# RWKV heads in one layout of full tiles: the second head's operands in reversed order, both heads' systems on the diagonal of one tile

## The chip, the cores and the metric

One core of a Trainium2 chip runs the whole program; the metric is device time in microseconds of one execution. PE in the rows is TensorE's matrix products, PEld its weight loads, DVE is VectorE, ACT ScalarE, POOL GpSimd, SP the engine whose queue issues the DMAs.

## What is computed

One residual layer over 16 learned and 1024 given tokens of 1024 channels, in float32. A normalised input goes through one projection of 61 tiles of 128 channels; three groups of heads mix over time; their outputs go through one output projection, a norm and the residual. The group in question is RWKV-7, 8 heads of 64 channels:

```python
def rwkv7_recurrence(r, w, k, v, a, b):          # (B, T, H, 64), state S (B, H, 64, 64)
    def step(state, inp):
        r_t, w_t, k_t, v_t, a_t, b_t = inp
        sa = jnp.einsum("bhvk,bhk->bhv", state, a_t)
        state = (state * w_t[:, :, None, :] + sa[..., None] * b_t[:, :, None, :]
                 + v_t[..., None] * k_t[:, :, None, :])
        return state, jnp.einsum("bhvk,bhk->bhv", state, r_t)
    ...
# called with a = -kk, b = kk * a, kk = l2_normalize(k * k_k) of each head
```

The others are gated DeltaNet (6 heads of 128) and Mamba-2 (12 heads of 64).

## The kernel before

**Projections.** A tile of 128 output channels takes 3 pieces of tokens x 8 blocks of input channels x 3 float32r products (high x high, high x low, low x high), 72 products `pj`. Its weights come by two DMAs, ScalarE rounds them (L149) and POOL computes the rest (L150); the next tile's weights are fetched when a tile has begun. Six `unit_a` (DeltaNet heads), four `unit_b` (pairs of RWKV heads) and two `unit_c` (Mamba) each project their tiles and then work them off in a scan over chunks; `unit_o` is the output projection.

**Order.** `schedule` writes out the order of all instructions by hand-made rules. Units are generators that yield after each step of a scan. A clock in microseconds of TensorE decides: when the result that a unit's next step waits for should be there, that step is emitted, otherwise the next product of a projection. `Meter` adds up the charges: a float32 product of n columns max(n, weight columns)/600 us, a projection product n/2400; and for the way back to TensorE, VectorE 0.25 + n/960, ScalarE 0.3 + n/1200 and POOL 0.3 + n/500 for n elements a partition, plus 0.3 a step. Instructions called through `nc.` are not charged. The plan is `a0 b0 b1 b2 c0 b3 a1 a2 a3 c1 a4 a5`. At most two scans run beside each other, each in a lane with two PSUM banks (`self.ps`). TensorE, like the other engines, takes what it was given in order.

**unit_b.** Chunks of 64 tokens, 17 of them; two heads lie on the partitions, 64 channels each. Per chunk `ar` = (a | r) and `bk` = (b | k) hold, along 128 columns, the operands of the token after and the token before, with their decays (VectorE). For each head a gram `bgm` (128 rows b, k by 128 columns a, r) is formed by one product of 64 rows and masked with `maskb`: four chunks a bank, a step for each head, ten steps. Its upper left 64x64 is a triangular system, scaled by `ib` = 1/|kappa|^2. The diagonal blocks of 32 go to DRAM and back to be solved (`solve32`), then pairs are merged to 64 by products of 32x32 (`bm`, through `bdd`), eight steps for two heads. Values are transposed into rows 64 to 127 of `uv`.

The scan has three steps a chunk. First `bsi` (bank `pq`): the state times `ar`, a full 128x128 product, then two products of 64x64 add k by a times the values for each head; ScalarE copies the upper half to `b_x`. Second `bu` (bank `pu`): two 64x64 products with the solved systems; VectorE scales the result by `ib` into rows 0 to 63 of `uv`. Third `bd`: a full product for the new state, which VectorE adds with the decay `b_wc` to what ScalarE has scaled (L817); and two products of 128 rows with 64 weight columns for the output, from `bgm` and `uv` into the lower half of `pq`, which ScalarE copies to `by` (L828).

Every call through a charged engine shows as L96, the line of `Meter`; go by the tile names.

## Time and profile before

| | |
|---|---|
| runs before (3) | 1534.42 us median, 1522.98 to 1535.38 |
| span of the profiled execution | 1518.0 us, first to last instruction; its own time outside the span is not listed |
| TensorE busy | 1427.0 us, 94% |
| VectorE, ScalarE, POOL busy | 1014.6, 647.8, 239.2 us |

Busy time of TensorE is the union of its products, whose ends are modelled; products overlap in the pipeline, so what one costs is seen in the distance between starts. A float32 product shows as two records, a float32r one as one.

### The profile page before, as it was taken

Reading aid. Unit: us, or ns where it says so; the run is one execution under the profiler, and the core shown is the slowest. Engines: PE = TensorE matmul, PEld = TensorE weight load, DVE = VectorE, ACT = ScalarE, POOL = GpSimd, SP = SyncE. Lnnn points to the kernel's source line nnn. Section 1 sums busy time; section 2 is a strip of 40 time slices with the busy share of each in tenths; the row PEclk is TensorE's granted clock in tenths of the full one; section 3 lists DMA queues with packets and bytes.
Section 4 is the critical chain, followed back from the end, with each engine's and each line's share of the span. In section 5 each row is a group of like instructions: output and inputs, shape, how many; then the busy total and the mean of one; then the engine's idle time right before and its main releaser. Section 6 shows DMA issues by size and latency. Waiting matters only on the chain.

```text
span 1518.0 us, 25931 instructions
## 1 busy us (share of the span) xinstructions
PE 1427.0 (94%) x9657; PEld 1259.6 (83%) x9657; DVE 1014.6 (67%) x2688; ACT 647.8 (43%) x1814; POOL 239.2 (16%) x227
## 2 busy tenths in 40 slices
PE   4999999999999999997999999999999999889897
PEld 3988878887888888987888898899998988678686
DVE  7549695476659456869735699745489967542573
ACT  5354351334434352443635534433456154532530
POOL 2122011011101111223101221102232111200100
PEclk9999998899999999999989999989999999999999
DMA  5221211111011121211111111101322111552851
GB/s 187 58 85 43 70 33 39 29 41 64 29 30 47 49 74 43 86 31 53 46 43 50 43 46 53 36 29 57 97 59 61 43 36 44 169 159 89 250 193 56
DMA packets 102880, 104.28 MB, mean 69 GB/s; under 512 B 37915, under 2 KB 70427, under 8 KB 102755
## 3 DMA queue, kind: packets, MB, share of 16 engines
q1 hardware_dynamic: 102755, 102.64, 22.0%
q8 instruction: 76, 1.25, 0.3%
q14 instruction: 49, 0.40, 0.1%
HBM read 85.00 MB, written 17.60 MB: 68 GB/s over the span
## 4 chain that ended last, share of the span: by engine, by line
PE 30%; DVE 14%; issue 5%; ACT 4%; DMA 3%; POOL 0%; SPq 0%; DVEq 0%; ACTq 0%; POOLq 0%
PE pj L96 14%; PE po L96 5%; DVE s_tmp L96 3%; DVE alb L96 2%; PE am L96 2%; DMA or<-in_w_out_dram 2%; PE bsi L96 1%; DVE aq L181 1%; DMA omrw<-d_mix 1%; PE aops L96 1%; PE ads L96 1%; DVE av L181 1%; PE aks L96 1%; PE av L96 1%; ACT clt L904 1%
## 5 line engine op out<-in xcount | busy, mean ns | idle before, releaser
L96 PE MATMUL pj<-hh,w 128*128 128x350 f32 (+8 forms) x2928 | 773.9, 338 | 0.2 <-ACT hh L261 0.2
L96 PEld LDWEIGHTS pj<-hh,w 128*128 128x128 f32 x2928 | 516.7, 192 | 13.2 <-issue 2.1
L96 PE MATMUL pj<-hl,w 128*128 128x350 f32 (+8 forms) x1464 | 493.4, 337 | 0.0
L150 POOL TENSOR_TENSOR w<-wr,w 128x512 fp32r<-128x512 f32 x122 | 173.6, 1424 | 870.3 <-ACT w L149 631.7
L96 PEld LDWEIGHTS pj<-hl,w 128*128 128x128 f32 x1464 | 281.3, 192 | 6.6 <-issue 0.9
L149 ACT CAST w<-wr 128x512 fp32r<-128x512 f32 x122 | 74.9, 615 | 75.8 <-PE pj L96 64.4
L96 PE MATMUL po<-ow,omw 128*128 128x512 f32 x408 | 95.5, 395 | 6.2 <-ACT omw L1064 3.7
L96 PEld LDWEIGHTS po<-ow,omw 128*128 128x128 f32 x408 | 77.2, 190 | 24.6 <-ACT omw L1064 4.4
L96 PE MATMUL po<-ow,ome 128*128 128x512 f32 x360 | 90.6, 399 | 4.6 <-ACT ow L1046 1.8
L96 PEld LDWEIGHTS po<-ow,ome 128*128 128x128 f32 x360 | 66.6, 188 | 20.1 <-POOL ow L1047 2.5
L96 DVE TENSOR_TENSOR alb<-alb,s_tmp 33x30 f32<-33x30 f32 (+9 forms) x180 | 71.2, 395 | 1.0
L96 DVE TENSOR_TENSOR s_tmp<-alb 33x30 f32<-33x30 f32 (+9 forms) x180 | 67.4, 375 | 0.9
L96 DVE TENSOR_TENSOR buv<-bu,b_ib 64x128 f32<-64x128 f32 x68 | 19.1, 281 | 69.5 <-PE bu L96 69.3
L96 PE MATMUL bsi<-buv,bgm 64*64 64x64 f32 (+1 forms) x528 | 61.5, 238 | 0.0
L96 PEld LDWEIGHTS bsi<-buv,bgm 64*64 64x64 f32 (+1 forms) x528 | 42.1, 139 | 17.5 <-issue 2.2
L828 ACT COPY by<-bsi 64x128 f32<-64x128 f32 x64 | 16.7, 262 | 82.3 <-PE bsi L96 81.8
L181 DVE SCALAR_TENSOR_TENSOR cbc<-pj,pack,cbc 128x346 f32<-128x346 f32 (+4 forms) x72 | 40.5, 568 | 14.3 <-ACT cbc L178 13.5
L96 DVE SCALAR_TENSOR_TENSOR b_s<-bd,b_wc,b_s 64x64 f32<-64x64 f32 x120 | 34.0, 283 | 23.2 <-PE bd L96 18.2
L96 DVE TENSOR_TENSOR blb<-blb,s_tmp 68x30 f32<-68x30 f32 (+14 forms) x120 | 46.5, 387 | 1.1
L96 PE MATMUL bgr<-bar,bbk 64*128 64x128 f32 x272 | 43.8, 328 | 2.6 <-DVE bbk L96 2.0
L1065 DVE TENSOR_TENSOR ome<-omre,ome 128x512 fp32r<-128x512 f32 (+2 forms) x40 | 22.4, 594 | 34.1 <-ACT ome L1064 34.0
L1047 POOL TENSOR_TENSOR ow<-or,ow 128x512 fp32r<-128x512 f32 x16 | 21.0, 1316 | 135.9 <-ACT ow L1046 135.9
(324 smaller groups left out, 2414.7 us busy)
## 6 DMA issues: line engine op xcount, KB each, us to landing
wr<-in_wt_dram SPq DMA_DIRECT2D x122, 256.0 KB, 2.6
or<-in_w_out_dram SPq DMA_DIRECT2D x32, 256.0 KB, 2.6
omrw<-d_mix SPq DMA_DIRECT2D x32, 256.0 KB, 4.7
clt<-d_cs SPq DMA_DIRECT2D x24, 256.0 KB, 4.5
omre<-d_mix SPq DMA_DIRECT2D x24, 256.0 KB, 4.2
btw<-d_tw SPq DMA_DIRECT2D x8, 544.0 KB
x<-in_x_dram SPq DMA_DIRECT2D x8, 512.0 KB, 7.0
oxr<-in_x_dram SPq DMA_DIRECT2D x8, 512.0 KB
```

Of the source, the lines that this page charges most:

```text
L96: return op(out, *args, **kw)
L149: nc.scalar.copy(w[:, 0], raw)
L150: nc.gpsimd.tensor_tensor(w[:, 1], raw, w[:, 0].bitcast(F32), SUB)
L181: nc.vector.scalar_tensor_tensor(acc[:, a + z: b], p[:, o + z - s: o + b - a - s], cw[:, 3 - s: 4 - s], acc[:, a + z: b], MUL, ADD)
L828: nc.scalar.copy(yt[hs[(c - 1) % 2], (c - 1) // 2, :], pq[64:128, 0:128])
L904: nc.scalar.activation(t[:, e, i], t[:, e, i], AF.Exp, bias=self.ncs[:, 1 + 4 * w + i, k + e: k + e + 1])
L1047: (nc.vector if k % 2 else nc.gpsimd).tensor_tensor(t[:, 1], raw, t[:, 0].bitcast(F32), SUB)
L1065: nc.vector.tensor_tensor(t[:, 1], raw, t[:, 0].bitcast(F32), SUB)
```

## The change

The first head of a pair keeps its order, the second has it reversed: `ar` is (a | r) on partitions 0 to 63 and (r | a) on 64 to 127, `bk` is (b | k) and (k | b). Gram products then are 64 rows by 64 weight columns by 128 columns, four a chunk instead of two, one for each quadrant of the array, into two banks: tile `bf` (program name `bgf`) holds what b meets, with both heads' systems on its diagonal; tile `be` (`bge`) what k meets. Each is masked with a mask of its own (`maskf`, `maske`, made once on POOL). Values stand off the diagonal of `uv`, which POOL clears first. A chunk's scan is five products of 128x128x128: `be` by `uv`, `ar` by the state, `bf` by `x`, `bt` by `uv`, and `bf` by the scaled `x` for the output. `x` is one of two cleared tiles `xb`; ScalarE writes its diagonal twice, first from `pq`, then scaled from `pu`, while VectorE writes the same solution to the diagonal of `uv`. Copies of diagonal parts are two instructions of 64x64 each. In the preparation the moves by halves are separate instructions, and r times its decay goes from VectorE to POOL. Merges take both heads in one step. Comments were removed throughout (not shown).

```diff
+masks = cp.tile([128, 2, 128], F32, tag="masks", name="masks")
+self.maskf, self.maske = masks[:, 0], masks[:, 1]
+lo, hi = slice(0, 64), slice(64, 128)
+for straight, turned, rows in ((self.maskf, self.maske, lo), (self.maske, self.maskf, hi)):
+    nc.gpsimd.tensor_copy(straight[rows], self.maskb[rows])
+    nc.gpsimd.tensor_copy(turned[rows, lo], self.maskb[rows, hi])
+    nc.gpsimd.tensor_copy(turned[rows, hi], self.maskb[rows, lo])
...
 ar, bk = ([self.one([128, 9 - i, 128], f"b{x}{p}_{i}") for i in range(2)] for x in ("ar", "bk"))
-ib = sm.tile([64, 17, 2], F32, tag="b_ib", name="b_ib")
+hs = (slice(0, 64), slice(64, 128))
+ib = sm.tile([128, 17], F32, tag="b_ib", name="b_ib")
 for i, (s, e) in enumerate(split):
     act.activation(bk[i][:, :, 0:64], k[:, s:e], AF.Square, scale=self.kk[:, p: p + 1])
 yield
 ps = self.ps(f"bn{p}")
 for c in range(17):
     pe.matmul(ps[0:64, 2 * c: 2 * c + 2], at_c(bk, c)[:, 0:64], self.blk[:, 0:65:64], start=True, stop=True)
-v.tensor_scalar(ib, ps[0:64, 0:34].rearrange("p (c h) -> p c h", h=2), EPS, None, ADD)
+for h in range(2):
+    v.tensor_scalar(ib[hs[h]], ps[0:64, h: 34: 2], EPS, None, ADD)
 v.reciprocal(ib, ib)
 for i, (s, e) in enumerate(split):
     kap, b_ = ar[i][:, :, 0:64], bk[i][:, :, 0:64]
     act.activation(kap, k[:, s:e], AF.Copy, scale=self.kk[:, p: p + 1])
     v.scalar_tensor_tensor(b_, at[:, s:e], 1.0, kap, ADD, MUL)
-    v.scalar_tensor_tensor(kap, kap, -1.0, e1[:, s:e, 0:64], MUL, MUL)
-    v.scalar_tensor_tensor(b_, b_, 0.5, cs[:, s:e, 1:], MUL, MUL)
+    for h in (1, 0):
+        v.scalar_tensor_tensor(ar[i][hs[h], :, hs[h]], kap[hs[h]], -1.0, e1[hs[h], s:e, 0:64], MUL, MUL)
+        v.scalar_tensor_tensor(bk[i][hs[h], :, hs[h]], b_[hs[h]], 0.5, cs[hs[h], s:e, 1:], MUL, MUL)
+        pool.tensor_tensor(ar[i][hs[h], :, hs[1 - h]], r[hs[h], s:e], e1[hs[h], s:e, 1:], MUL)
...
 for i, (s, e) in enumerate(split):
-    v.tensor_tensor(bk[i][:, :, 64:], k[:, s:e], cs[:, s:e, 1:], MUL)
-    v.tensor_tensor(ar[i][:, :, 64:], r[:, s:e], e1[:, s:e, 1:], MUL)
+    for h in range(2):
+        v.tensor_tensor(bk[i][hs[h], :, hs[1 - h]], k[hs[h], s:e], cs[hs[h], s:e, 1:], MUL)
 yield 11
 self.calm = False
-gms = [[self.one([128, 9 - i, 128], f"bgm{p}_{h}{i}") for i in range(2)] for h in range(2)]
-gm = lambda h, c: at_c(gms[h], c)
+bf, be = ([self.one([128, 9 - i, 128], f"b{x}{p}_{i}") for i in range(2)] for x in ("gf", "ge"))
 banks = ((1, 5), (5, 9), (9, 13), (13, 17), (0, 1))
-hs = (slice(0, 64), slice(64, 128))
 for s, e in banks:
-    for h in range(2):
-        ps = self.ps(f"bgr{p}_{h}{s}")
-        for c in range(s, e):
-            pe.matmul(ps[:, 128 * (c - s): 128 * (c - s) + 128], at_c(bk, c)[hs[h]], at_c(ar, c)[hs[h]], start=True, stop=True)
-        v.tensor_tensor(gms[h][s // 9][:, s % 9: s % 9 + e - s, :], ps[:, : 128 * (e - s)].rearrange("p (c t) -> p c t", c=e - s),
-                        bc(self.maskb, 1, e - s), MUL)
-        yield PIPE
+    pf, pg = self.ps(f"bgf{p}_{s}"), self.ps(f"bge{p}_{s}")
+    for c in range(s, e):
+        to = slice(128 * (c - s), 128 * (c - s) + 128)
+        for out, row, h in ((pf, 0, 0), (pf, 1, 1), (pg, 0, 1), (pg, 1, 0)):
+            pe.matmul(out[hs[row], to], at_c(bk, c)[hs[h], hs[row]], at_c(ar, c)[hs[h]], start=True, stop=True)
+    for out, ps, mask in ((bf, pf, self.maskf), (be, pg, self.maske)):
+        v.tensor_tensor(out[s // 9][:, s % 9: s % 9 + e - s, :], ps[:, : 128 * (e - s)].rearrange("p (c t) -> p c t", c=e - s),
+                        bc(mask, 1, e - s), MUL)
+    yield PIPE
 for h in range(2):
     for i, (s, e) in enumerate(split):
-        ab = gms[h][i][0:64, :, 0:64]
-        nc.vector.tensor_tensor(ab, ab, bc(ib[:, s:e, h], 2, 64), MUL)
+        ab = bf[i][hs[h], :, hs[h]]
+        nc.vector.tensor_tensor(ab, ab, bc(ib[hs[h], s:e], 2, 64), MUL)
...
-blocks = [(34 * h + 17 * b + s, e - s, gms[h][i][32 * b: 32 * b + 32, :, 32 * b: 32 * b + 32])
-          for h in range(2) for b in range(2) for i, (s, e) in enumerate(split)]
+quarter = [slice(32 * b, 32 * b + 32) for b in range(4)]
+blocks = [(17 * b + s, e - s, bf[i][quarter[b], :, quarter[b]]) for b in range(4) for i, (s, e) in enumerate(split)]
...
 uv = [self.one([128, 9 - i, 128], f"buv{p}_{i}") for i in range(2)]
+for t in uv:
+    nc.gpsimd.memset(t, 0.0)
 for c in range(0, 17, 4):
     cc = range(max(c - 3, 0), c + 1)
+    n = max(len(cc) // 2, 1)
     ps = self.ps(f"bvT{p}_{c}")
-    for j in range(0, len(cc), 2):
-        pe.transpose(ps[: 64 * min(2, len(cc)), 64 * j: 64 * j + 128], v_[:, 64 * cc[j]: 64 * (cc[j] + min(2, len(cc)))], ident)
-    for j, x in enumerate(cc):
-        h = slice(64 * (j % 2), 64 * (j % 2) + 64)
-        act.copy(at_c(uv, x)[64:128], ps[h, 64 * (j - j % 2): 64 * (j - j % 2) + 128])
+    for j in range(n):
+        w = 64 * min(2, len(cc))
+        pe.transpose(ps[:w, 128 * j: 128 * j + 128], v_[:, 64 * cc[2 * j]: 64 * cc[2 * j] + w], ident)
+    pairs = ps[:, : 128 * n].rearrange("p (j t) -> p j t", j=n)
+    for j in range(min(2, len(cc))):
+        x = cc[j]
+        for h in range(2):
+            act.copy(uv[x // 9][hs[1 - h], x % 9: x % 9 + 2 * n - 1: 2, hs[h]], pairs[hs[j], :, hs[h]])
...
-dv = self.one([128, 34, 32], f"bdd{p}")
-f, s = slice(0, 32), slice(32, 64)
-for h in range(2):
+dv = self.one([128, 17, 32], f"bdd{p}")
+fs = [(quarter[2 * h], quarter[2 * h + 1]) for h in range(2)]
+for f, _ in fs:
     for i, (c0, c1) in enumerate(split):
-        nc.vector.transpose(dv[f, 17 * h + c0: 17 * h + c1, :], gms[h][i][f, :, f])
+        nc.vector.transpose(dv[f, c0: c1, :], bf[i][f, :, f])
 self.lag += 4
 yield
-for i0, n in ((0, 9), (9, 8), (17, 9), (26, 8)):
-    p1 = self.ps(f"bm1{p}_{i0}")
-    for i in range(i0, i0 + n):
-        pe.matmul(p1[s, 32 * (i - i0): 32 * (i - i0) + 32], gm(i // 17, i % 17)[f, s], dv[f, i, :], start=True, stop=True)
-    act.copy(dv[s, i0: i0 + n, :], p1[s, : 32 * n].rearrange("p (c t) -> p c t", c=n))
+for i, (c0, c1) in enumerate(split):
+    p1 = [self.ps(f"bm1{p}_{i}{h}") for h in range(2)]
+    for c in range(c1 - c0):
+        for (f, s), ps in zip(fs, p1):
+            pe.matmul(ps[s, 32 * c: 32 * c + 32], bf[i][f, c, s], dv[f, c0 + c, :], start=True, stop=True)
+    for (f, s), ps in zip(fs, p1):
+        act.copy(dv[s, c0: c1, :], ps[s, : 32 * (c1 - c0)].rearrange("p (c t) -> p c t", c=c1 - c0))
     yield
-    p2 = self.ps(f"bm2{p}_{i0}")
-    for i in range(i0, i0 + n):
-        pe.matmul(p2[f, 32 * (i - i0): 32 * (i - i0) + 32], dv[s, i, :], gm(i // 17, i % 17)[s, s], start=True, stop=True)
-    act.copy(gms[i0 // 17][n % 9 // 8][f, :, s], p2[f, : 32 * n].rearrange("p (c t) -> p c t", c=n))
+    p2 = [self.ps(f"bm2{p}_{i}{h}") for h in range(2)]
+    for c in range(c1 - c0):
+        for (f, s), ps in zip(fs, p2):
+            pe.matmul(ps[f, 32 * c: 32 * c + 32], dv[s, c0 + c, :], bf[i][s, c, s], start=True, stop=True)
+    for (f, s), ps in zip(fs, p2):
+        act.copy(bf[i][f, :, s], ps[f, : 32 * (c1 - c0)].rearrange("p (c t) -> p c t", c=c1 - c0))
     yield 0.1
...
 yt = self.one([128, 8, 128], f"by{p}")
+xb = [sm.tile([128, 128], F32, tag="bx", name=f"bx{p}_{i}", bufs=4) for i in range(2)]
+for x in xb:
+    nc.gpsimd.memset(x, 0.0)
 st = None
 for c in range(17):
     pq = self.ps(f"bsi{p}_{c}")
+    pe.matmul(pq[:, 0:128], at_c(be, c), at_c(uv, c), start=True, stop=(c == 0), skip_group_check=True)
     if c:
-        pe.matmul(pq[:, 0:128], at_c(ar, c), st, start=True, stop=False, skip_group_check=True)
+        pe.matmul(pq[:, 0:128], at_c(ar, c), st, start=False, stop=True, skip_group_check=True)
+    x = xb[c % 2]
     for h in range(2):
-        pe.matmul(pq[0:64, hs[h]], gm(h, c)[64:128, 0:64], at_c(uv, c)[64:128, hs[h]],
-                  start=(c == 0), stop=True, skip_group_check=True)
-    x = self.tmp("b_x")
-    act.copy(x[0:64], pq[0:64, 0:128])
+        act.copy(x[hs[h], hs[h]], pq[hs[h], hs[h]])
     yield
     pu = self.ps(f"bu{p}_{c}")
+    pe.matmul(pu[:, 0:128], at_c(bf, c), x, start=True, stop=True)
     for h in range(2):
-        pe.matmul(pu[0:64, hs[h]], gm(h, c)[0:64, 0:64], x[0:64, hs[h]], start=True, stop=True)
-    v.tensor_tensor(at_c(uv, c)[0:64].rearrange("p (h d) -> p h d", h=2), pu[0:64, 0:128].rearrange("p (h d) -> p h d", h=2),
-                    bc(ib[:, c, :], 2, 64), MUL)
+        v.tensor_scalar(at_c(uv, c)[hs[h], hs[h]], pu[hs[h], hs[h]], ib[hs[h], c: c + 1], None, MUL)
+    if c:
+        for h in range(2):
+            nc.scalar.activation(x[hs[h], hs[h]], pu[hs[h], hs[h]], AF.Copy, scale=ib[hs[h], c: c + 1])
     yield
     if c < 16:
         pd = self.ps(f"bd{p}_{c}")
...
             for h in range(2):
                 v.tensor_scalar(sn[hs[h], hs[h]], pd[hs[h], hs[h]], wc[hs[h], c + 1: c + 2], None, MUL)
     if c:
+        pe.matmul(pq[:, 0:128], at_c(bf, c), x, start=False, stop=True, skip_group_check=True)
         for h in range(2):
-            pe.matmul(pq[64:128, hs[h]], gm(h, c)[:, 64:128], at_c(uv, c)[:, hs[h]],
-                      start=False, stop=True, skip_group_check=True)
-        nc.scalar.copy(yt[hs[(c - 1) % 2], (c - 1) // 2, :], pq[64:128, 0:128])
+            nc.scalar.copy(yt[hs[(c - 1) % 2], (c - 1) // 2, hs[h]], pq[hs[1 - h], hs[h]])
         self.lag = max(0.2, self.lag - 0.21)
```

## Rows read from the trace of the kernel before

**Rows 1.** The page's head: span, then busy us, share and instructions by engine.

```profile
span 1518.0 us, 25931 instructions
...
PE 1427.0 (94%) x9657; PEld 1259.6 (83%) x9657; DVE 1014.6 (67%) x2688; ACT 647.8 (43%) x1814; POOL 239.2 (16%) x227
```

**Rows 2.** Stages: length, busy us of PE, PEld, DVE, ACT, POOL; granted clock.

```profile
260.00:420.00 160.00, 158.52 (x1101) 134.23 (x1101) 100.05 (x247) 61.45 (x158) 17.21 (x17) 0.90 0.13 39
420.00:600.00 180.00, 176.92 (x1325) 153.56 (x1324) 115.35 (x297) 72.63 (x203) 23.45 (x24) 1.00 0.17 48
600.00:700.00 100.00, 92.85 (x641) 87.67 (x641) 82.33 (x191) 46.25 (x134) 24.14 (x23) 1.00 0.20 61
...
780.00:870.00 90.00, 90.00 (x616) 77.15 (x615) 47.27 (x156) 47.88 (x173) 14.36 (x16) 0.96 0.13 39
870.00:1030.00 160.00, 154.50 (x1111) 142.09 (x1110) 121.84 (x348) 66.23 (x196) 26.05 (x21) 0.96 0.13 41
```

**Rows 3.** TensorE in order of time: start us, length, product, records.

```profile
803.51 0.38 PE L96 MATMUL ads<-a_vn,akd 128*128 128x128 f32 x2
803.73 0.39 PE L96 MATMUL aops<-a_s,aq 128*128 128x128 f32 x2
803.96 0.39 PE L96 MATMUL aops<-a_vn,aup 128*128 128x128 f32 x2
804.10 0.56 PE L96 MATMUL pj<-hh,w 128*128 128x348 f32 x2
```

**Rows 4.** TensorE in order of time, inside an RWKV scan.

```profile
838.75 0.44 PE L96 MATMUL bu<-b_x,bgm 64*64 64x64 f32 x4
839.12 0.43 PE L96 MATMUL pj<-hh,w 128*128 128x348 f32 x1
839.39 0.32 PE L96 MATMUL pj<-hl,w 128*128 128x348 f32 x1
839.55 0.32 PE L96 MATMUL pj<-hh,w 128*128 128x348 f32 x1
839.71 0.39 PE L96 MATMUL bd<-buv,bbt 128*128 128x128 f32 x2
840.02 0.45 PE L96 MATMUL bsi<-buv,bgm 128*64 128x64 f32 x4
840.40 0.42 PE L96 MATMUL pj<-hh,w 128*128 128x348 f32 x1
840.66 0.32 PE L96 MATMUL pj<-hl,w 128*128 128x348 f32 x1
```

**Rows 5.** Groups of TensorE's instructions by form: records, busy us, mean ns.

```profile
L96 PE MATMUL bu<-b_x,bgm 64*64 64x64 f32 x272 | 31.4, 236 | 0.0
```

**Rows 6.** What TensorE's weight loads waited for: us, times, longest.

```profile
PEld bu L96 <- ACT b_x L96: 5.0, 25, 0.3
PEld bu L96 <- ACT b_s L817: 4.9, 22, 0.3
```

**Rows 7.** Instructions on the tile `b_s`: ns shortest/median/longest.

```profile
L96 DVE TENSOR_SCALAR b_s<-bd,b_wc x8: 266/283/291, 267.7 to 778.0; 64x64 f32<-64x64 f32 x8
```

**Rows 8.** Groups of ScalarE's instructions by form: busy us, mean ns.

```profile
L96 ACT COPY b_x<-bsi 64x128 f32<-64x128 f32 x68 | 17.5, 257 | 53.7 <-PE bsi L96 53.0
L96 ACT ACTIVATE a_vn<-av,a_nbd 128x128 f32<-128x128 f32 x48 | 17.5, 364 | 18.3 <-PE av L96 17.8
```

**Rows 9.** TensorE in order of time: grams of two heads, then of one.

```profile
155.02 1.71 PE L96 MATMUL bgr<-bar,bbk 64*128 64x128 f32 x16
...
162.30 1.16 PE L96 MATMUL bgr<-bar,bbk 64*128 64x128 f32 x8
```

**Rows 10.** All engines in order of time, 237.5 to 239.9 us.

```profile
237.46 1.74 POOL L150 TENSOR_TENSOR w<-wr,w 128x512 fp32r<-128x512 f32 x1
...
237.97 1.77 DVE L96 SCALAR_TENSOR_TENSOR bbk<-bbk,bcs 128x512 f32<-128x512 f32 x1
```

**Rows 11.** Instructions on the tile `bbk`: ns shortest/median/longest.

```profile
L96 DVE SCALAR_TENSOR_TENSOR bbk<-bbk,bcs x8: 673/745/1774, 134.6 to 664.0; 128x576 f32<-128x576 f32 x4, 128x512 f32<-128x512 f32 x4
```

## The prediction

> **What bounds the kernel now.** I read the page's head first, then a table of engine time by stage, then single instructions of TensorE in order of time. The head says 1518.0 us of span and TensorE at work for 94% of it [rows 1]. The table says where this holds without a gap: in the three stretches that hold the RWKV scans, TensorE is idle for 1.5 us of 160, 3.1 of 180 and 0.0 of 90, while VectorE works 100, 115 and 47 us in them [rows 2]. So in a scan stretch a microsecond of TensorE is a microsecond of the kernel: an excursion to a scan product pushes back the projection products (`pj`) behind it. ScalarE at 61 of 160 us is far from a bound there. The two other stretches in the group show what happens where VectorE is fuller: with 82 of 100 us TensorE loses 7.2 us, with 122 of 160 it loses 5.5.
>
> How long does a scan product hold TensorE? Its busy time doesn't tell, because pipelined products overlap; the distance between starts does. In a run of full-array products (weights 128x128, 128 columns) starts are 0.22 us apart: 803.51, 803.73, 803.96, then the projection at 804.10 [rows 3]. Each float32 product shows as two records, so x2 is one product. In the scan it looks otherwise [rows 4]. `bd` (full array) starts at 839.71 and the half-width products `bsi` behind it only at 840.02: 0.31, where 0.22 was due, so 0.09 is lost on the way in. The two `bsi` take until 840.40; then the first projection product takes 0.26 (840.40 to 840.66), where the next one takes 0.16 (839.39 to 839.55). TensorE thus pays at each change between whole-array and part-array products, in both directions. From `bd` to the second projection product are 0.95 us; less that product's 0.16, the excursion costs **0.79**. The excursion of two `bu` products (64x64) takes 838.75 to 839.39 less 0.16, 0.48, and with the 0.09 of the way in **0.57**.
>
> **The change, part by part.** All of it is in the unit of an RWKV head pair; there are 4 units of 17 chunks, 68 chunks (272 records of `bu` are 136 products, two a chunk [rows 5]).
>
> (1) *Scan products.* A chunk has three excursions before: state product and two half products (the shape of `bd` and `bsi`, 0.79), two `bu` (0.57), `bd` and two half products (0.79): 2.15 us. After: five full-array products with no change of shape, 5 x 0.22 = 1.11. That is 1.04 less for 64 chunks, and for the first chunk of a unit, which has no state and no output, 0.57 + 0.57 + 0.22 against 3 x 0.22, 0.69 less: 67 + 3 = **-69 us** (1.04 is 2.15 - 1.11). In columns nothing is saved (2 full and 6 half-width products against 5 full ones); it is all in the changes of shape.
>
> (2) *A new wait on ScalarE.* The last product of a chunk reads the solution from `x`, written by two new ScalarE instructions, where it read what VectorE wrote before; and `bd` writes a bank that these two must have read (each of the two scan lanes has two banks). Behind both on TensorE's queue stand all projections. The wait that the trace has of this kind is that of `bu` for ScalarE's copy: 25 times 5.0 us in all and 22 times 4.9, so 9.9 us for 68 chunks, 0.15 a chunk [rows 6]. One to two more such hops give 10 to 20 us; I take **+15**. Below that end lies 0 (VectorE's own two instructions may end later anyway).
>
> (3) *Longer steps of the chain.* VectorE's write of the solution becomes two instructions of 64x64; one takes 0.283 [rows 7], so a step is 0.28 us longer. The planner's own charge rises by 0.25 (2 x (0.25 + 64/960) against 0.25 + 128/960), so it puts as many more projection products in between. ScalarE's copy of 0.257 becomes two, each below that [rows 8]; the charge rises by 0.30. Output copies double likewise, off the chain; the two scaled writes are at most 0.364 each, the price of a scaled 128x128 [rows 8]. ScalarE gets at most 68 x (2 x 0.364 + 2 x 0.257) = 84 us more, and has room for it. VectorE gets 68 x 0.283 = 19 us here, plus 4 units x 4 more instructions of the preparation (each moved by halves of the partitions, which take no less time than whole ones, so some 0.7 us): 30 us in all. In the scan stretches (430 us now, some 375 then) VectorE's share goes from 61% (263 of 430) to 78% (293 of 375). At 76% TensorE lost 3.4% of a stretch, at 82% 7.2%; it loses 1.1% there now. So 2.3 to 6.1% of 375 us are 9 to 23; I take **+15**.
>
> (4) *Grams.* 34 products a unit with 128 weight columns become 68 with 64 weight columns, each still streaming 128 columns. If they come one after another, 68 x 0.22 = 15 us a unit, against now 34 x 0.19 (eight products in x16 records: 1.71 less the last one's 0.27 is 1.44, and one more step of 0.11 makes 1.55 [rows 9]). The number of steps falls from ten to five, each spared excursion saves some 0.3 in changes of shape (0.57 less two products of 0.11 is 0.35; some adjoin others already), 1.5 a unit. So serial: 15.0 - 6.6 - 1.5 = 6.9 a unit, +28. But the rows show that products on different halves of the rows overlap: eight records of one head need (1.16 - 0.27)/7 = 0.127 a step, sixteen records, eight of either head, (1.71 - 0.27)/15 = 0.096, which is less than the 0.11 that 128 columns take in a whole array [rows 9]. The new order alternates the halves, so I take pairs: 7.5 - 6.6 - 1.5 = -0.6 a unit, **-2**. The other end is all four quadrants at once: 3.7 - 6.6 - 1.5 = -4.4 a unit, -18. On this the Trainium skill, "TensorEngine Tiling (Array Packing)", section "Key Properties", says that different tiles work independently and can load and multiply in parallel; by it the sum would be 16 us lower than mine. The rows show it for halves of the rows, none shows it for halves of the columns.
>
> (5) *Merges.* As many products, in 4 steps where there were 8: 4 spared excursions of 0.3 x 4 units, **-5**. The copies of values, the transposes, the block DMAs (eight each way on SP's queue) keep their number and shape; the memsets of `uv` and `xb` go to POOL ahead of the scans, where it is idle most of the time (17 of 160 us busy [rows 2]) and the next weights are a projection ahead: 0.
>
> (6) *r on POOL.* Per unit four products move from VectorE's two to POOL. POOL's 128x512 product took 1.74 us, so 16 of them are at most 28 us of POOL; weights that wait behind them were fetched a projection tile earlier (72 products of 0.16, 11.5 us). While that POOL product ran, a VectorE instruction with two SBUF inputs took 1.77 [rows 10], where the quickest of its kind took 0.673 [rows 11]. The Trainium skill, "SBUF — State Buffer", section "Who interferes with whom", says that a VectorE instruction with two SBUF inputs contends with a GpSimd one that reads SBUF; this row agrees. So up to 16 x 1.1 = 18 us of VectorE, in the preparation, under projection products; I take **+3**, ends 0 and 18. Where that cover is gone, the grams start later by up to 4.4 us a unit.
>
> Sum: -69 + 15 + 15 - 2 - 5 + 3 = **-43 us**. The profiled execution gives a span of 1518.0, so 1475 there; what lies around it is not listed, and the median of the runs is 16.4 above the span. I take that off the median: 1534 - 43 = **1491**.
>
> **The rivals.**
> *Grams one after another* (28 where I put -2): 1521. For it: a step holds 16 short products where it held 4, and no row has two quadrants side by side. Against it: the overlap of the halves in rows 9.
> *Four quadrants at once* (-18): 1475. For it only the page's rule above.
> *The changes of shape were covered*: the planner puts a product where it expects a result, and with TensorE quicker the chain through ScalarE and VectorE ends last anyway. Then the time stays at 1534. Against it: no idle time in the scan stretches.
> *Slower: ScalarE ahead of the third step.* TensorE's queue is in order; `bd` and the last product now stand behind two ScalarE instructions that queue among the evictions of the projections. It decides against the change once TensorE waits over 1.04 us a chunk, seven times the 0.15 of rows 6. At 1.3 a chunk the scan would cost 0.26 x 68 = 18 more than before: 1552. For it: six ScalarE instructions a chunk where two were. Against it: ScalarE is busy 38% of the first scan stretch.
> *It does not do what it says*: if a full-array product took the price of a part-array one even without a change of shape, the gain would go too; rows 3 exclude that, and it is in the third rival's chance.
>
> **How the numbers follow.** Forecast (with its waits anywhere between the ends of 2, 3 and 6) 0.55; grams in series 0.15; four at once 0.12; covered 0.10; slower 0.08. The first stretch had a granted clock of 0.90 [rows 2], so some 32 of its 160 us at the lower of two levels; if other stretches fall, that is up to 16 us either way, inside the range. The range leaves out the last two: downward the four-quadrant case with the small ends of (2) and (3), about 1462; upward the series case with part of the large ends, 1530. One per cent, 15 us, is about what can be told from no change: the runs before lie 12 us apart. Faster by over 1% (below 1519): forecast and four at once, and the better part of the series case, 0.73; within 1%: the rest of the series case, the covered one, 0.19; slower by over 1%: 0.08.
>
> **What would show it.** In the changed profile: no half-width products in the scan, and starts 0.22 apart at the five; projection products 0.16 apart right behind them; TensorE's idle time in scan stretches 3 to 6%, with ScalarE's scaled write of `x` (step 2) or VectorE (step 3) as what ended it; sixteen gram products of a bank (x32) in about 1.9 us (pairs), 3.7 (series) or 1.0 (four); VectorE near 78% in those stretches. I would be wrong if waits for ScalarE in the third step come to over half a microsecond a chunk, or if the new order of the planner opens gaps late in the kernel, where no row speaks for it.

## The result and the profile after

The changed kernel takes **1590.9 us** (median of 4 runs, 1586.0 to 1592.7) beside 1529.5 of the kernel before (4 runs, 1523.0 to 1535.4): ratio **1.038**, 95% interval 1.033 to 1.043. The forecast was 1491, the range 1462 to 1530. It is 61 us slower, and no rival had this time. Medians here and below leave out the three runs, two of e12 and one of e14, that fell in a slower state of the chip.

The page's head after: span, then busy us, share and instructions of each engine (beside [rows 1]).

```profile
span 1590.9 us, 26124 instructions
...
PE 1436.3 (90%) x9529; PEld 1253.5 (79%) x9529; DVE 1068.9 (67%) x2776; ACT 710.1 (45%) x2078; POOL 263.1 (17%) x265
```

TensorE has 128 records less and is busy no shorter; its share falls from 94% to 90%. The stage table says where (columns as in [rows 2]); the last three lines are narrower windows.

```profile
260.00:420.00 160.00, 152.34 (x1165) 128.76 (x1163) 117.94 (x267) 78.26 (x223) 27.85 (x27) 0.97 0.15 45
420.00:600.00 180.00, 152.73 (x972) 130.85 (x972) 124.31 (x296) 74.83 (x225) 30.79 (x29) 0.88 0.16 44
780.00:870.00 90.00, 58.94 (x510) 51.38 (x510) 68.97 (x233) 26.27 (x79) 9.89 (x12) 0.82 0.16 42
870.00:1030.00 160.00, 155.88 (x1120) 135.87 (x1119) 92.92 (x276) 88.16 (x301) 20.96 (x21) 0.95 0.12 38
...
500.00:540.00 40.00, 24.98 (x169) 18.84 (x170) 26.29 (x58) 12.27 (x31) 0.65 (x4) 0.60 0.23 61
760.00:775.00 15.00, 4.63 (x19) 3.16 (x18) 14.87 (x40) 5.59 (x21) 2.65 (x3) 0.63 0.08 29
803.00:833.00 30.00, 0.48 (x2) 0.22 (x3) 28.12 (x103) 3.99 (x13) 0.63 (x4) 0.53 0.07 17
```

Where the four scans run (277 to 374, 420 to 505, 629 to 722, 901 to 996 us, by the first and last `bu`) TensorE is still busy for 89 to 98% of the time. Most of the loss lies **between** them: 27 us of the stretch from 420 to 600, 31 of the 90 from 780 to 870, and with each hole the granted clock falls to the lower of its two levels (0.50 is 1.2 GHz). Over the whole span the mean clock is 0.937, so 2 x 0.063 x 1591 = 200 us at the lower level; in the kernel before it was 0.970, 92 us.

What is missing in the first hole is shown by the same table for the projection products alone (tile `pj`; no POOL column):

```profile
420.00:500.00 80.00, 49.93 (x242) 37.60 (x241) 12.40 (x23) 7.64 (x15) 0.96 0.08 24
500.00:540.00 40.00, 2.41 (x5) 1.27 (x5) 6.47 (x14) 3.70 (x8) 0.60 0.23 61
```

242 records of projections in 80 us, then 5 in 40: next to none stand on TensorE's queue there. What ended the hole at 803 us, in order of time, and one group of VectorE's work in it (ns shortest/median/longest):

```profile
832.90 0.66 PE L96 MATMUL aqT<-pack,aq 128*128 128x128 f32 x2 [27.22 <-DVE aq L184]
```

```profile
L96 DVE TENSOR_TENSOR s_tmp<-blb x24: 188/356/395, 813.0 to 839.6; 68x168 f32<-68x168 f32 x2, 68x184 f32<-68x184 f32 x2, 68x198 f32<-68x198 f32 x2, 68x210 f32<-68x210 f32 x2
```

The substitution of an RWKV pair (`blb`) and that of a DeltaNet head (`alb`) share VectorE, and the eviction of `aq`, which TensorE's next product needs, stands behind both: 27.2 us without a product. Such a meeting isn't new, only its length. In the kernel before it cost 9.6 us; in e1 below, which has the changed instructions planned as before, 16.1; in e2, which has the old instructions planned as after, 32.8 (TensorE in order of time, one line of each):

```profile
720.71 0.66 PE L96 MATMUL avT<-pack,av 128*128 128x128 f32 x2 [9.60 <-DVE av L184]
730.43 0.66 PE L98 MATMUL avT<-pack,av 128*128 128x128 f32 x2 [16.09 <-DVE alb L98]
797.31 0.66 PE L98 MATMUL aqT<-pack,aq 128*128 128x128 f32 x2 [32.84 <-DVE aq L186]
```

So this hole is a matter of **order**, not of an instruction's price: with the old instructions it is no shorter.

The scan itself. All engines in order of time, from a chunk of the third scan (lines of other tiles left out):

```profile
649.81 0.41 ACT L96 COPY bx<-bsi 64x64 f32<-64x64 f32 x2
...
650.27 0.49 PE L96 MATMUL bu<-bx,bgf 128*128 128x128 f32 x2
...
650.80 0.28 DVE L96 TENSOR_SCALAR buv<-bu,b_ib 64x64 f32<-64x64 f32 x1
...
651.18 0.29 DVE L96 TENSOR_SCALAR buv<-bu,b_ib 64x64 f32<-64x64 f32 x1
...
651.57 0.64 ACT L840 ACTIVATE bx<-bu,b_ib 64x64 f32<-64x64 f32 x2
...
652.26 0.30 PEld L96 LDWEIGHTS bd<-buv,bbt 128*128 128x128 f32 x2 [0.39 <-ACT bx L840]
```

VectorE's two reads of the bank `bu` come first, and only when the second is done (651.47) does ScalarE begin its two; `bd`, which overwrites that bank, waits for these until 652.26. So the new ScalarE writes don't lie beside VectorE's but behind them. Over the kernel, what TensorE's weight loads waited for (us in all, times, longest; beside [rows 6]), and ScalarE's group (busy, mean ns, idle before it and what ended it):

```profile
PEld bd L96 <- ACT bx L840: 22.1, 45, 2.0
PEld bu L96 <- ACT bx L96: 17.6, 53, 0.8
PEld bsi L96 <- ACT by L857: 15.6, 45, 0.8
```

```profile
L840 ACT ACTIVATE bx<-bu,b_ib 64x64 f32<-64x64 f32 x128 | 39.5, 308 | 50.2 <-DVE buv L96 48.2
```

22.1 + 17.6 + 15.6 is 55.3 us, 0.81 a chunk where the rows of before give 0.15. The Trainium skill, "PSUM — Partial Sum Buffer", section "PSUM bank collisions raise a hardware error", says that two engines must not be in the same bank and quadrant of partitions at once, and that one guards by bank and quadrant (by bank is the simple version), not by address; the 48.2 us that ScalarE stood waiting for VectorE's reads agree with a program that is guarded so.

What this does to the price of a chunk on TensorE shows when every excursion with projection products on both sides is reckoned as in the prediction (from the start of the projection product in front to that of the second one behind, less two of 0.158 us; medians, with the number of cases). Before: `bu` 0.57 (38), `bd` with the output 0.80 (37), the products of `bsi` 0.80 (35), together 2.17. Changed: `bu` 0.53 (46), `bd` with the output 0.81 (40), the two products of `bsi` in one excursion 0.74 (20), together **2.08**, where 1.11 was forecast. The cheapest case of each kind took 0.23, 0.45 and 0.46, which is 1.14: the forecast's price exists, but nearly every excursion waits. Of the 68 `bu`, 55 start 0.05 us after the end of ScalarE's second copy, as above (649.81 + 0.41 is 650.22, and `bu` starts at 650.27); in the kernel before 2 of 68 do, and in the middle case the operand had been there for 0.31 us. A case of that kind, from the kernel before:

```profile
287.84 0.26 ACT L96 COPY b_x<-bsi 64x128 f32<-64x128 f32 x1
...
288.51 0.44 PE L96 MATMUL bu<-b_x,bgm 64*64 64x64 f32 x4
```

### The profile page after: what moved, and what is told of

The parts are those of the page before. It is cut to its first block, busy times and chain, and to the rows that moved or that the text cites. A ratio compares the mean times of both kernels' runs of the same rounds, so it can differ in the third digit from the quotient of the medians.

```text
span 1590.9 us, 26124 instructions
## 1 busy us (share of the span) xinstructions
PE 1436.3 (90%) x9529; PEld 1253.5 (79%) x9529; DVE 1068.9 (67%) x2776; ACT 710.1 (45%) x2078; POOL 263.1 (17%) x265
## 5 line engine op out<-in xcount | busy, mean ns | idle before, releaser
L96 PE MATMUL pj<-hh,w 128*128 128x350 f32 (+8 forms) x2928 | 783.3, 341 | 0.2 <-ACT hh L261 0.2
L96 PEld LDWEIGHTS pj<-hh,w 128*128 128x128 f32 x2928 | 523.5, 195 | 7.2 <-issue 4.1
L150 POOL TENSOR_TENSOR w<-wr,w 128x512 fp32r<-128x512 f32 x122 | 165.4, 1357 | 817.3 <-ACT w L149 682.6
L96 DVE TENSOR_SCALAR buv<-bu,b_ib 64x64 f32<-64x64 f32 x136 | 38.5, 283 | 83.6 <-PE bu L96 77.7
L96 DVE TENSOR_TENSOR s_tmp<-alb 33x30 f32<-33x30 f32 (+9 forms) x180 | 72.4, 402 | 5.2 <-DMA alb<-d_m 4.0
L840 ACT ACTIVATE bx<-bu,b_ib 64x64 f32<-64x64 f32 x128 | 39.5, 308 | 50.2 <-DVE buv L96 48.2
L96 DVE TENSOR_TENSOR s_tmp<-blb 68x30 f32<-68x30 f32 (+14 forms) x120 | 45.8, 382 | 4.7 <-DMA blb<-d_l 3.6
L181 DVE SCALAR_TENSOR_TENSOR cx<-pj,pack,cx 128x346 f32<-128x346 f32 (+2 forms) x54 | 30.5, 573 | 19.4 <-ACT cx L178 18.6
L857 ACT COPY by<-bsi 64x64 f32<-64x64 f32 x128 | 26.5, 207 | 35.1 <-PE bsi L96 33.9
```

The lines of the kernel that those rows point to most:

```text
L96: return op(out, *args, **kw)
L150: nc.gpsimd.tensor_tensor(w[:, 1], raw, w[:, 0].bitcast(F32), SUB)
L181: nc.vector.scalar_tensor_tensor(acc[:, a + z: b], p[:, o + z - s: o + b - a - s], cw[:, 3 - s: 4 - s], acc[:, a + z: b], MUL, ADD)
L840: nc.scalar.activation(x[hs[h], hs[h]], pu[hs[h], hs[h]], AF.Copy, scale=ib[hs[h], c: c + 1])
L857: nc.scalar.copy(yt[hs[(c - 1) % 2], (c - 1) // 2, hs[h]], pq[hs[1 - h], hs[h]])
```

## The experiments

Medians in us; the kernel before, run beside them on the same chip, had 1530 to 1533. "Order" is the order in which the program's planner emits the units' parts; it depends on what each part's instructions are charged (VectorE 0.25 us + columns/960, ScalarE 0.3 + columns/1200, POOL 0.3 + columns/500) and on how many steps a part has. The planner is not the last to decide, though it looks so from its description: `kernel.py` gives its steps priorities (`tc.high_priority`), and TensorE's sequence in the traces is another than the planner's. Ahead of the last `bu` of the second scan stand 1374 projection products in the kernel before and 1464 in e1, which is planned like it; 1608 in the changed kernel and 1593 in e3, whose edit the planner doesn't see. "The same order" therefore means the same planning, and a difference between two such runs still holds a shift of TensorE's sequence.

**e1, changed instructions in the order of before.** Steps of grams and merges as before, and the charges of the old instructions.

```diff
+        self.free = True
         for h in range(2):
             act.copy(x[hs[h], hs[h]], pq[hs[h], hs[h]])
+        self.free = False
+        self.lag += 0.3 + 128 / 1200
```

> The new instructions, but steps and charges of the planner as before the change, so that it emits the order of before. If the order alone made the loss, the forecast holds here: 1485 to 1500 us. If the two ScalarE writes of x in each chunk made it, the order doesn't help: 1560 to 1595. If both count (the scan's saved changes of shape, 69 us, against some 47 us more waits for ScalarE that the changed trace shows), 1505 to 1530.

Measured **1533.9**, ratio 0.9996 [0.9964, 1.0028], in none of the three ranges, nearest to both causes together. **e2, instructions of before in the order of after**, the same the other way round:

```diff
+            self.lag += 0.3
             yield
             pu = self.ps(f"bu{p}_{c}")
```

> The old instructions in the steps and with the charges of the changed kernel, so that the planner emits the new order (ten gram steps become five, eight merge steps four, scan steps charged 0.25 to 0.3 us more). If the order made the loss: 1575 to 1600 us. If the waits for ScalarE made it: 1525 to 1540.

Measured **1551.4**, 1.0101 [1.0048, 1.0154], between its two ranges. So order takes 57 of the 61 us from the changed kernel, but costs the old instructions only 18: the two don't add.

**e3 and e4, without ScalarE's second write of `x`**, in the order of after and of before. The output product reads `uv`, so y is another sum than the reference's.

```diff
-                for h in range(2):
-                    nc.scalar.activation(x[hs[h], hs[h]], pu[hs[h], hs[h]], AF.Copy, scale=ib[hs[h], c: c + 1])
...
-                pe.matmul(pq[:, 0:128], at_c(bf, c), x, start=False, stop=True, skip_group_check=True)
+                pe.matmul(pq[:, 0:128], at_c(bf, c), at_c(uv, c), start=False, stop=True, skip_group_check=True)
```

> The changed kernel without ScalarE's second write of x: the output product reads uv instead, which holds the values beside the solution, so y gets a wrong term; the planner doesn't charge these writes, so the order stays. The state product bd then waits for VectorE alone. If the waits for ScalarE made the loss: 1530 to 1560 us. If the order made it: 1580 to 1592.

> Both: order of before, and no second write of x (same wrong term in y). If the two causes add up and nothing else was wrong with the forecast: 1465 to 1490 us. If changes of shape in the scan cost less than the rows said, over 1505.

Measured **1569.3** and **1512.1** (ratios 1.0231 [1.0211, 1.0250], 0.9870 [0.9843, 0.9898]): 22 us less than with the write, in either order. e3 lies between its ranges; e4 lies where its expectation had the changes of shape cost less than the rows said. The prices of a chunk above give another reading: they are gone, but waits have taken their place.

**e5, the output product a step later.** e1 with the output product and its copies at the head of the next chunk, and ScalarE's copy taken from `uv` in SBUF, so that nothing but VectorE reads the bank `bu`; the whole computation.

```diff
+            if c > 1:
+                finish(c - 1, old)
...
-                    nc.scalar.activation(x[hs[h], hs[h]], pu[hs[h], hs[h]], AF.Copy, scale=ib[hs[h], c: c + 1])
+                    nc.scalar.copy(x[hs[h], hs[h]], at_c(uv, c)[hs[h], hs[h]])
```

> The new instructions in the order of before, but the output product and its two copies stand at the head of the next chunk's first step, and ScalarE copies the scaled solution from uv instead of reading the bank of bu, so that neither bd nor the next chunk's first product waits for ScalarE; the same result. If the three waits for ScalarE a chunk are what ate the saved changes of shape, the waits of bd and bsi for ScalarE go (some 30 us) and the time is 1495 to 1512 us, where the same order without this took 1534. If the scan's waits don't decide, 1528 to 1540.

Measured **1514.2**, 0.9873 [0.9843, 0.9903], 20 us less than e1 and as good as leaving the write out, 2 us above its range. Its weight loads of `bd` wait for ScalarE no more; these two waits stay:

```profile
PEld bu L98 <- ACT bx L90: 16.7, 48, 1.6
PEld bsi L98 <- ACT by L842: 11.4, 35, 0.7
```

**e6, only the scan's charges of before** in the changed kernel (the edit shown for e1, and its like at `uv`).

> The changed kernel with the planner's charges for the two scan steps as before the change (0.30 and 0.25 us less a chunk), its gram and merge steps as changed. If the scan's charges make the bad order, 1530 to 1555 us; if the grams and merges taken together in one step do, 1575 to 1595.

Measured **1597.1**, 1.0418 [1.0380, 1.0456]: not the scan's charges by themselves. **e7, the kernel before with another allowance** of the planner, to see what order alone can do.

```diff
-LOOK, LATE, EVAC, DMA = 0.05, 0.3, 2.0, 5.0
+LOOK, LATE, EVAC, DMA = 0.05, 0.35, 2.0, 5.0
```

> The kernel before with 0.05 us more of allowance a step in the planner (0.35 for 0.30), nothing else: how much the time depends on the order alone, with no change that matters. If the order before was one among many like it, within 10 us of 1533; if it is a lucky one, 1545 to 1570.

Measured **1514.7**, 0.9876 [0.9831, 0.9921], outside both ranges: 0.05 us more a step, no instruction changed, 17 us gained. A difference of that size between two orders says nothing of the instructions.

**e8, r back on VectorE** in e5.

```diff
-                pool.tensor_tensor(ar[i][hs[h], :, hs[1 - h]], r[hs[h], s:e], e1[hs[h], s:e, 1:], MUL)
+                v.tensor_tensor(ar[i][hs[h], :, hs[1 - h]], r[hs[h], s:e], e1[hs[h], s:e, 1:], MUL)
```

> As the first, with r times its decay back on VectorE (four instructions a unit, by halves). If POOL's part costs by delaying VectorE or the weights, 3 to 10 us less than the first; if it is covered, within 3 us of it.

Measured **1524.1**, 0.9954 [0.9926, 0.9983], 10 us above e5, outside both ranges. These are four instructions by halves a unit; the kernel before had two whole ones.

**e9, only the preparation's charges of before** (the reciprocal, the moves by halves, r on POOL); every instruction and step as changed.

```diff
+            self.free = True
             for h in (1, 0):
                 v.scalar_tensor_tensor(ar[i][hs[h], :, hs[h]], kap[hs[h]], -1.0, e1[hs[h], s:e, 0:64], MUL, MUL)
...
                 pool.tensor_tensor(ar[i][hs[h], :, hs[1 - h]], r[hs[h], s:e], e1[hs[h], s:e, 1:], MUL)
+            self.free = False
+            self.lag += 2 * (0.25 + 64 * (e - s) / 960)
```

> The changed kernel, every instruction and every step as changed; only what the planner is told of the preparation (the reciprocal, the moves by halves of the partitions and r on POOL) is the kernel before's charge. Theory, the planner runs out of projections: the changed charges delay a pair's preparation in the planner's clock until the next units' tiles no longer fit beside it, and a scan is emitted with no projection to fill it. The planner's own clock jumps over 58 us without work in the changed kernel, over 14 with this edit, over 10 in the kernel before; so about 44 us come back: 1540 to 1555. Rival, the fewer and longer steps of grams and merges cost the time: 1575 to 1595, no change against the changed kernel.

Measured **1551.8**, 1.0115 [1.0049, 1.0181], as the theory had it. **e10, the charges of e6 and e9 together** (both edits), grams and merges in the changed steps and with the charges of these.

> As the run before, with the two charges of the scan also as before (those alone gave 1597); grams and merges stay in the changed steps. Theory: the planner's clock jumps over 10 us as before, so the time is that of the changed instructions in the order of before, 1530 to 1540, and the steps of grams and merges are worth under 10 us either way. Rival (the steps cost the time): 1565 to 1595.

Measured **1530.5**, 0.9998 [0.9967, 1.0029], as the theory had it. **e11, the reverse**: e1 with the edit of e9 taken out.

> The other way round: scan charges, gram steps and merge steps as before, only the preparation is charged as in the changed kernel. Theory: this charge alone brings the gaps back (the planner's clock jumps over 38 us, 28 more than before), so 1555 to 1575 where all charges and steps of before gave 1534. Rival (the steps of grams and merges): 1530 to 1540.

Measured **1604.5**, 1.0466 [1.0405, 1.0528]: 71 us for charges alone. The direction is the theory's; the size is more than twice what it had from the planner's clock. Stage tables of e1 and of e11 (columns as above), then e11's projection products in its first two scans:

```profile
420.00:600.00 180.00, 163.94 (x1151) 136.49 (x1148) 123.33 (x319) 98.36 (x309) 24.67 (x29) 0.97 0.13 38
...
780.00:870.00 90.00, 87.56 (x616) 75.63 (x613) 54.69 (x180) 61.35 (x227) 13.53 (x15) 0.94 0.14 41
870.00:1030.00 160.00, 155.46 (x1070) 139.97 (x1070) 111.31 (x323) 68.17 (x207) 24.07 (x21) 0.91 0.13 39
```

```profile
420.00:600.00 180.00, 150.63 (x1017) 122.82 (x1017) 101.09 (x255) 80.17 (x255) 21.14 (x22) 0.85 0.10 28
...
780.00:870.00 90.00, 78.86 (x572) 66.99 (x571) 58.41 (x186) 38.68 (x143) 11.86 (x14) 0.81 0.21 59
870.00:1030.00 160.00, 134.98 (x992) 120.64 (x991) 104.20 (x330) 62.01 (x206) 41.72 (x21) 0.85 0.12 36
```

```profile
279.00:362.00 83.00, 54.09 (x265) 41.67 (x266) 22.60 (x42) 12.29 (x24) 1.00 0.10 30
441.00:520.00 79.00, 22.88 (x109) 16.70 (x109) 3.11 (x7) 2.87 (x7) 0.83 0.08 21
```

Against e1, e11 loses 13 and 9 us of TensorE in two stretches where the changed kernel loses too, and 20 in a third, where that one is nearly full; the clocks are 0.81 to 0.85. Its second scan takes as long as the first (79 and 83 us) with 109 records of projections where the first has 265: the chain sets its length, and what it doesn't cover is lost. The 20 us of the third stretch are something else, one hole that e6 has at the same length:

```profile
913.21 0.66 PE L98 MATMUL pj<-hh,w 128*128 128x348 f32 x1 [23.61 <-DVE cbc L186]
```

Here a projection product does stand next on the queue. It waits for VectorE's eviction `cbc`, and from 889 to 914 us VectorE is busy without a break, 85 of its 88 instructions belonging to the substitution `alb`. The planner charges each unit for itself and doesn't know that two units share VectorE; its 28 us more don't hold this hole, which goes some way to the excess.

**e12, e5 with the allowance of e7.**

> The version with the output product a step later and the scaled copy taken from SBUF (1514 beside 1531), and the planner's allowance LATE at 0.35 for 0.30, which alone took 17 us from the kernel before. If both gains stand by themselves: 1495 to 1500. If the allowance only moved the order of that one kernel to a better place: anywhere from 1505 to 1525, no better than without it.

Measured **1517.2**, 0.9894 [0.9843, 0.9944], no better than e5: the allowance's gain was that order's own.

**e13, no product reads `x`.** e4 with one line more; the system is left unsolved, and as `bu` no longer needs `bsi`, the chain from one chunk to the next is cut as well.

```diff
-            pe.matmul(pu[:, 0:128], at_c(bf, c), x, start=True, stop=True)
+            pe.matmul(pu[:, 0:128], at_c(bf, c), at_c(uv, c), start=True, stop=True)
```

> The changed instructions in the order of before, without ScalarE's scaled copy, and both products that read `x` read `uv` instead: `x` is still written, nobody reads it, so the result is not the reference's (the system isn't solved for what it should be). No product of the scan then waits for ScalarE's `x`. If the spared changes of shape are worth what step 1 says and only the waits on ScalarE ate them, the two hops take about 40 us from 1534: 1485 to 1500 beside 1532. If full-array products cost about what the part-array ones did, it stays where the version without the scaled copy was: 1505 to 1520.

Measured **1481.5**, 0.9679 [0.9628, 0.9729], 4 us under its range. TensorE in order of time shows what step 1 had drawn:

```profile
311.65 0.38 PE L98 MATMUL bsi<-b_s,bar 128*128 128x128 f32 x2
311.87 0.39 PE L98 MATMUL bu<-buv,bgf 128*128 128x128 f32 x2
312.01 0.39 PE L98 MATMUL pj<-hl,w 128*128 128x322 f32 x1
```

Starts are 0.22 and 0.14 apart. Of the weight loads' waits for ScalarE one is left:

```profile
PEld bsi L98 <- ACT by L873: 12.0, 35, 0.7
```

**e14, e5 with the changed steps of grams and merges** (the edit of e5 in e10), with the charges of these.

> The version with the output product a step later, now with the grams and merges in the changed (fewer, longer) steps and only the charges of scan and preparation as before. If these steps are worth 5 us as the prediction's step 5 has it: 1505 to 1512. If they are neutral, as 1530 beside 1534 says: 1510 to 1518. If fewer steps leave TensorE worse filled: 1520 to 1535.

Measured **1525.5**, 0.9962 [0.9934, 0.9991]: worse than e5 by 11, while e10 and e1 agree within 4. The steps have no price of their own that shows above what orders differ by.

Side by side, in us:

| instructions | order of before | order of after |
|---|---|---|
| those of before | 1530 to 1533 | 1551 (e2) |
| changed | 1534 (e1) | 1591 |
| changed, without the second write of `x` | 1512 (e4) | 1569 (e3) |
| changed, no product waits for `x` | 1481 (e13) | not run |

## Why the prediction was wrong

**The step that failed** is step 3 with the cover in step 6: "the planner's own charge rises by 0.25, so it puts as many more projection products in between", and the preparation's work "under projection products". I took the order as given and the charges as a help. They have no term in the sum, and they cost 57 us (1591 against e1's 1534). The decisive charges are those of the preparation (39 us, e9), and once these are back the scan's are worth 21 more (e10 against e9). A pair has five more VectorE instructions, one of them for `ib`, and four POOL products to wait for in the planner's clock: 9.0 us by the rates given, of which 5.6 are POOL's, added to VectorE's as if the one came after the other. Its grams come later there, and its tiles are held longer. With 26 tiles in all, 12 of them held by one pair, 8 to 9 by the next and the rest by the Mamba unit, no further projection fits, and in the planner's order a scan or a solve goes out with nothing beside it; on TensorE's queue the lack shows behind the second scan, from 500 to 540 us. By the planner's own clock it is 58 us without work in the changed kernel, 10 in the one before. e9, e10 and e11 show the charges on the chip from both sides; that the tile budget is the link was read from the planner's state and not varied. It can be the link only for the holes that lack projections. The longest single holes (27.2 us here, 23.6 in e11 and e6) are waits for VectorE behind a substitution, a result of the new order that the planner's clock doesn't contain. The prediction's last sentence named gaps of the planner as a sign of being wrong, "late in the kernel", and gave them no chance, because "no row speaks for it": no row can, since the order after isn't in the trace of before.

**Step 2 was mis-sized** as well: 15 us stood for waits that eat nearly all of step 1's 69. By the prices of a chunk they come to 2.08 - 1.14, 0.94 us, which over 64 chunks is an estimated 60 us; by the rows of weight loads to 0.81. e1, which has them and not the order, lies 43 us above the forecast. Singly, `bd`'s is worth about 22 (e4 against e1, e5 shows it without leaving work out); `bu`'s up to 31 (e13 against e4; e13 also cuts the chain, so this is an upper end); the wait for the output copies stays at 11 to 16 in the rows of the changed kernel, e5 and e13. [rows 6] priced one copy behind one product at 0.15 us (its second row is a wait for the scaled state, L817, not for the copy, and as 66 of the 68 `bu` of the kernel before start well after the copy's end, the rows can hold little waiting for it); here `bu` waits for two copies in a row, and `bd` for two reads behind two VectorE reads of one bank. The rival of ScalarE ahead of the third step had the mechanism; all three waits together, 0.81 to 0.94 us a chunk, stay just under the 1.04 from which it would decide, and in the order of before they leave nothing of step 1's gain (1534 against 1533). The third step alone has 22.1 us, 0.33 a chunk, under the half microsecond that was named as a sign.

**Step 1 was right about the price of a product that finds its operand ready**, and wrong in taking that for the usual case. Without two of the three waits, and with the chain cut, the changed products bring 48 us (e13 against before), of -69 forecast; 12 us are still waited for the output copies there. Only two of the 46 `bu` cost 0.23; this is one of them, TensorE in order of time, from the changed kernel's third scan:

```profile
643.54 0.32 PE L96 MATMUL pj<-hl,w 128*128 128x342 f32 x1
643.70 0.39 PE L96 MATMUL bu<-bx,bgf 128*128 128x128 f32 x2
643.85 0.55 PE L96 MATMUL pj<-hh,w 128*128 128x342 f32 x2
644.24 0.32 PE L96 MATMUL pj<-hl,w 128*128 128x340 f32 x1
```

From 643.54 to 644.24 are 0.70 us; less three projection products of 0.157 (x2 are two), 0.23 are left for `bu`. Where it waits, as at 650.27 above, the products around it start at 649.89 and 650.91, and the same sum gives 0.55, the usual case, about what the part-array excursion of [rows 4] took (0.57).

**Step 3's VectorE term** can't be told from the order: VectorE is busy for 58 to 77% of the four wide windows, where the step had 78% of the scans. It is the bound in the holes, with 28 of 30 us at 803.

**Step 4 was right**: pairs. In order of time, first and last of one bank pair's 32 records:

```profile
786.83 0.76 PE L96 MATMUL bgf<-bar,bbk 64*64 64x128 f32 x9
...
787.82 0.60 PE L96 MATMUL bge<-bar,bbk 64*64 64x128 f32 x8
```

787.82 + 0.60 - 786.83 is 1.59 us for 16 products, where [rows 9] has 1.71 for 8 with twice the weight columns; pairs were forecast at about 1.9, series at 3.7, four at once at 1.0. The Trainium skill, "TensorEngine Tiling (Array Packing)", section "Key Properties", has different tiles multiply in parallel; the rows show that for two here, not for four.

**Step 5** (-5) doesn't show (e10, e14). **Step 6** had a range of 0 to 18 us of loss; r on POOL is 10 us better than on VectorE by halves (e8 against e5), less than orders differ by, but no loss. The POOL products sum to 21 us (16 x 1.30), and the weights queued behind them do wait for these, 20 us in four places, as the form of waiting that step 6 named; group and waiters:

```profile
L96 POOL TENSOR_TENSOR bar<-br,be x16: 1183/1302/1709, 120.0 to 739.1; 64x576 f32<-64x576 f32 x8, 64x512 f32<-64x512 f32 x8
```

```profile
  POOL w L150: 20.0, 4
```

Why the order of after costs the old instructions 18 us and the changed ones 57 isn't settled. In the order of before the changed instructions without the second write gain 20 us, in that of after they lose 18 (1569 against 1551). That fits TensorE being the bound in one and the chains in the other, since saved TensorE time is worth nothing in a hole and a longer step is; but no run separates it, and TensorE's sequence isn't the same in e2 and the changed kernel either.

One reading of the prediction was off and cost nothing: the 16.4 us between span and median don't lie around the span. The profiled runs since lie 1.7 to 2.1 us above their own spans; the rest is spread between runs.

## What to carry to other kernels

In a program that plans its own order, a change of charges or steps is a change of its own: build it with the old order first (here one flag), and take differences of one or two per cent between orders as scatter. Before an engine gets a second read of a PSUM bank, ask which reads it will stand behind and which product overwrites the bank; here taking the copy from SBUF and using it a step later turned 1534 into 1514, 1.3% below the kernel before, which the old instructions reach too with another allowance (e7). When an instruction becomes two, look at how long its result now lies ready before the product that reads it: 0.31 us of slack was all that kept `bu` from waiting. Spared TensorE time counts only while projections are there to fill it.

## What the runs showed of the hardware that was not expected

Gram products in 64x64 tiles, alternating between halves of rows and of columns, end 32 records in 1.59 us, half the time a record of [rows 9]. And a hole seems to cost twice: in 813 to 832 us, where TensorE has no product at all, its granted clock is 0.50, and 220 of e11's 1600 us (2 x 0.069 x 1600) lie at the lower level, against 113 of e1's 1532 (2 x 0.037 x 1532). With the same 9529 records TensorE is busy for 1408 us in e1, 1436 in the changed kernel and 1452 in e11. That fits products inside and behind holes running at the lower level, but nothing separates it from their being packed otherwise. Behind the hole of 27.2 us the projection products stand 0.29 apart for some 3 us and 0.16 after that, so little is paid there.
